# A streaming-encoder block on eight cores: the last down projection in two token ranges, and the wait for the stores moved behind the last branch

## The chip, the cores and the metric

The kernel runs on all 8 cores of one Trainium2 chip. Each core computes one of eight batch elements, with no exchange between cores. The metric is the device time of the slowest core, in microseconds (us). In code and profile lines PE is TensorE, PEld its weight loads, DVE VectorE, ACT ScalarE, POOL GpSimd and SP SyncE; a q behind the name means the engine's queue.

The program has a slow state: in some executions the cores of one die, or of both, get a lower clock, and the time rises by up to 19% (the kernel before once took 3316.71 us). All comparisons here use fast runs. Where I compare cores, I use only dies whose four cores all had a granted clock of 0.99 or more; I call these undisturbed.

## The reference, cut to what matters

```python
# x: (8, 4096, 1024) float32
x = x + 0.5 * swiglu(rmsnorm(x, norm_ffn1), ...)         # first feed-forward half
x = x + merged_attention_and_gating(rmsnorm(x, norm_mix)) @ w_out
x = x + 0.5 * swiglu(rmsnorm(x, norm_ffn2), w_gate, w_up, w_down)
return rmsnorm(x, norm_final)                            # g * x * rsqrt(mean(x*x) + eps)
```

Each core takes its 4096 tokens in 8 tiles of 512. For the last tile nothing is left after the second feed-forward but the final norm and the stores.

## The kernel before, the parts concerned

The program is recorded as a list of operations for each engine. A tracker keeps, for each named resource, its last writer and readers, and turns conflicts into semaphore waits. The resource of the residual is `("X", buffer, d)`: 128 features of all 512 tokens.

```python
def nsq(t, d, eng="pool"):         # squares, summed over the 8 feature blocks
    ... ACT Square -> TG;  eng: ACC += TG  (d == 7: DVE, ACCR = ACC + TG)
def nstat():                       # sum over features, then rsqrt as exp(-0.5 ln)
    ... PE ONESR.T @ ACCR -> psum; ACT Ln -> RSTD; ACT Exp -> RSTD
def napply(t, which, d):           # DVE: X = X * g * RSTD
def store(t, d):                   # SP: rows d and d+1 of X to DRAM

def down(t, i, fac, hook, ...):
    for d in range(8):
        W, wres, k = get_slot(("wds", i, d))
        by = dense_bank()                      # one of four PSUM banks
        ... 22 matmuls of 512 columns into bank(by)
        ... DVE: X[d] = bank(by) * fac + X[d]
        free_slot(k)
        hook()                                 # here nsq(t, d)

# the end of the fast path
run_all(ffn(t, 1, False, ffn2_hooks(t)))
if last:
    nstat()
    for d in range(8):
        napply(t, 3, d)
        if d % 2:
            store(t, d - 1)
outs = [("outd", d) for d in range(0, 8, 2)]
p.add("sp", lambda e: e.nop(), reads=outs)     # SyncE waits for the stores here
p.branch(cond, ["FLI"])                        # every engine reads a flag; if the fast path
...                                            # was not valid, a general version runs
```

The arm after the branch is normally not taken, but all its instructions lie between the branch and the end of the program. So each engine ends with a jump over them. Below, the evict of a block is the VectorE instruction that adds its PSUM bank to the residual (the line with `* fac`), and the issue of a store is the moment at which its queue sends it off.

Of the kernel before, what the change touches and what calls it, by code (L numbers as in the profile page):

```python
# [10 lines left out]
AF = mybir.ActivationFunctionType  # L11
ALU = mybir.AluOpType
# [5 lines left out]
T = 512  # L18
NT = S_LEN // T
NGR = 46  # L20
NSEM = 12
EPS = 1e-6
R_MAX = 1e18
BIAS_MAX = 10.0
# [36 lines left out]
class Prog:  # L61
    ENGS = ("pe", "act", "dve", "pool", "sp")

    def __init__(self, nc):
        self.nc = nc
        self.ops = {e: [] for e in self.ENGS}
        self.last_writer = {}
        self.readers = {}
        self.dma_counts = {}

    @staticmethod
    def _halves(keys):
# [47 lines left out]
    def dma(self, queue, fn, reads=(), writes=(), sem=None, paced=False):  # L120
# [10 lines left out]
        self.ops[queue].append(op)  # L131
        return op

    def branch(self, cond, reads):

        for e in self.ENGS:
            op = _Op(e, cond)
            op.branch = True
            op.idx = len(self.ops[e])
            self._track(op, reads, ())  # L140
            self.ops[e].append(op)

    def emit(self):
        nc = self.nc
        for e in self.ENGS:
            c = 0
            for op in self.ops[e]:
                if not op.is_dma:
                    op.semkey = ("eng", e)
                    if op.signal:  # L150
                        assert not op.branch
                        c += 1
                        op.count = c
        semkeys = [("eng", e) for e in self.ENGS] + [("dma", k) for k in self.dma_counts]
        with ExitStack() as st:
            sems = {k: st.enter_context(nc.semaphore("s_" + "_".join(str(x) for x in k))) for k in semkeys}
            block = st.enter_context(nc.Block())
            engmap = {"pe": block.tensor, "act": block.scalar, "dve": block.vector,
                      "pool": block.gpsimd, "sp": block.sync}

            def make(e):
                def body(eng):
                    waited = {}
                    with ExitStack() as arm:
                        for op in self.ops[e]:
                            for d in op.deps:
                                if waited.get(d.semkey, 0) >= d.count:
                                    continue
                                eng.wait_ge(sems[d.semkey], d.count)
                                waited[d.semkey] = d.count  # L170
                            if op.branch:
                                arm.enter_context(eng.If(op.fn(eng)))
                                continue
                            inst = op.fn(eng)
                            if op.is_dma:
                                inst.then_inc(sems[op.semkey], 16)
                            elif op.signal:
                                inst.then_inc(sems[op.semkey], 1)
                return body

            for e in self.ENGS:
                if self.ops[e]:
                    engmap[e](make(e))
# [19 lines left out]
def build_nc(n_tiles=NT):  # L203
# [28 lines left out]
    with ExitStack() as st:  # L232
# [5 lines left out]
        def bank(i):  # L238
            return PS[i // 2][:, (i % 2) * 512:(i % 2 + 1) * 512]

        def rb(i):
            return ("ps", i)
# [53 lines left out]
        def run(p, dry):  # L296
# [85 lines left out]
            def free_slot(k):  # L382
                if not dry:
                    del live[k]
                    pump()
# [14 lines left out]
            def dense_bank():  # L400
                b = dn[0] % n_dense[0]
                dn[0] += 1
                return b
# [60 lines left out]
                p.add("dve", lambda e: e.memset(EB[64:128, h0:h0 + 2, 0:64], 0.0), reads=[("EB", i)], writes=[("EB", i)])  # L464
                p.add("dve", lambda e: e.memset(EB[0:64, h0:h0 + 2, 576:640], 0.0), reads=[("EB", i)], writes=[("EB", i)])

            def nsq(t, d, eng="pool"):
                src, xres = X[t % 3][:, d, :], ("X", t % 3, d)
                if d == 0:
                    p.add("act", lambda e: e.activation(out=ACC[:], in_=src, func=AF.Square, scale=1.0 / 32.0),  # L470
                          reads=[xres], writes=["ACC"])
                    return
                buf, bres = tg_buf()
                p.add("act", lambda e: e.activation(out=buf[:], in_=src, func=AF.Square, scale=1.0 / 32.0),  # L474
                      reads=[xres], writes=[bres])
                if d < 7:
                    p.add(eng, lambda e: e.tensor_tensor(out=ACC[:], in0=ACC[:], in1=buf[:], op=ALU.add),  # L477
                          reads=["ACC", bres], writes=["ACC"])
                else:
                    p.add("dve", lambda e: e.tensor_tensor(out=ACCR[:], in0=ACC[:], in1=buf[:], op=ALU.add),  # L480
                          reads=["ACC", bres], writes=["ACCR"])

            nb = [0]

            def nstat(dst=RSTD[:], dres="RSTD"):
                b = 6 + nb[0] % 2
                nb[0] += 1
                p.add("pe", lambda e: e.matmul(bank(b), lhsT=ONESR[:], rhs=ACCR[:], start=True, stop=True),
                      reads=["ACCR", "ONESR"], writes=[rb(b)])
                p.add("act", lambda e: e.activation(out=dst, in_=bank(b), func=AF.Ln, bias=EPSB[:]),  # L490
                      reads=[rb(b), "EPSB"], writes=[dres])
                p.add("act", lambda e: e.activation(out=dst, in_=dst, func=AF.Exp, scale=-0.5),  # L492
                      reads=[dres], writes=[dres])

            def napply(t, which, d):
                xres = ("X", t % 3, d)
                src = X[t % 3][:, d, :]
                dst, dres = (XT[t % 2][:, d, :], ("XT", t % 2, d)) if which < 3 else (src, xres)
                p.add("dve", lambda e: e.scalar_tensor_tensor(  # L499
                    out=dst, in0=src, scalar=G4[:, which * 8 + d:which * 8 + d + 1], in1=RSTD[:], op0=ALU.mult, op1=ALU.mult),  # L500
                    reads=[xres, "RSTD", "G4"], writes=[dres])

            def nraw(t, which, d):
# [1 line left out]
                    out=XT[t % 2][:, d, :], in0=X[t % 3][:, d, :], scalar1=G4[:, which * 8 + d:which * 8 + d + 1],  # L505
                    scalar2=None, op0=ALU.mult), reads=[("X", t % 3, d), "G4"], writes=[("XT", t % 2, d)])

            def store(t, d):
                b = t % 3
                p.dma("sp", lambda e: e.dma_start(out=out_d[:, d:d + 2, t * T:(t + 1) * T], in_=X[b][:, d:d + 2, :]),  # L510
                      reads=[("X", b, d), ("X", b, d + 1)], writes=[("outd", d)], sem=f"o{d}")

            N_FFN = 2 * NFC + 16

# [115 lines left out]
                        hook()  # L630
                        yield

            def ffn(t, i, use_tanh, hooks=None, narrow=False):
                hook = Hooks(hooks)
                for f2 in F2:
                    yield from gu_chunk(t, f2, get_slot(("ffs", i, f2)), "tanh" if use_tanh else "silu", hook)
                yield from down(t, i, 0.25 if use_tanh else 0.5, hook, narrow=2 * narrow)

            def gate_up_both(hooks):

# [382 lines left out]
            def ffn2_hooks(t):  # L1023
                hk = {}
                if t + 1 < n_tiles:
                    for s in range(4):
                        add_hook(hk, 8 + 3 * s, P(sgu_mix, t + 1, s))
                if t + 2 < n_tiles:
                    for d in range(8):
                        add_hook(hk, 10 + 3 * d, P(nsq, t + 2, d, "dve" if t == 0 else "pool"))  # L1030
                    add_hook(hk, 40, nstat)
                    for d in range(8):
                        add_hook(hk, D1 + d, P(napply, t + 2, 0, d))
                if t == n_tiles - 1:
                    for d in range(8):
                        add_hook(hk, 4 + 2 * d, P(nsq, t - 1, d))
                    finish_hooks(hk, t - 1, 22)
                    add_hook(hk, 38, flag_ops)
                if t != n_tiles - 2:
                    for d in range(8):  # L1040
                        add_hook(hk, D1 + 2 * d + 1, P(nsq, t, d))
                return hk

            def run_all(g):
                for _ in g:
                    pass
# [29 lines left out]
            for t in range(n_tiles):  # L1076
# [32 lines left out]
                if t == n_tiles - 2:  # L1109
                    last_ffn = ffn(t, 1, True, ffn2_hooks(t), narrow=True)  # L1110
                    interleave(last_ffn, attention(t + 1), N_FFN + 16 - 8, n_att(t + 1), 2 * NFC)
                else:
                    run_all(ffn(t, 1, False, ffn2_hooks(t)))
                    if last:
                        nstat()
                        for d in range(8):
                            napply(t, 3, d)
                            if d % 2:
                                store(t, d - 1)
                    else:  # L1120
                        pass
            outs = [("outd", d) for d in range(0, 8, 2)]
            p.add("sp", lambda e: e.nop(), reads=outs)

            def cond(e):
                r = e.alloc_register("flag")
# [109 lines left out]
```

## Time and profile before

| | us |
|---|---|
| listed runs before the change | 3316.71, 2795.04, 2960.86 (the first and third in the slow state) |
| its profiled execution | 2789.63, cores' spans 2777.5 to 2786.6 |
| first matmul of the last down projection to end of span, median of cores | 57.7 |
| of that, the projection itself | 38.4 |
| last matmul to last store's issue | 11.4 |
| last store's issue to end of span | 7.9 |

The span runs from a core's first to its last recorded instruction. The last four rows are my local measure and its parts, taken from the trace of the profiled execution on all eight cores; it varies by some 0.3 us between most cores, while whole spans of undisturbed cores differ by about 3 us (standard deviation). The local measure starts at the first weight load of the projection. The lines of the profile that carry the reading stand in the prediction.

### The profile page before, as it was taken

How to read it: one execution, taken by the hardware profiler on the slowest of the kernel's cores; microseconds unless marked ns; L12 is line 12 of the kernel's file. 1: busy time of each engine (PE TensorE's matmuls, PEld its weight loads, DVE VectorE, ACT ScalarE, POOL GpSimd, SP SyncE). 2: the span in 40 equal slices, each digit the busy share in tenths (PEclk: the TensorE clock that was granted, in tenths of full speed). 3: DMA queues.
4: the chain of work that ended last, by engine and by line, in shares of the span. 5: the costliest groups of instructions: out<-in, count | busy, mean ns of one | idle time of the engine just before them, and what ended most of it. 6: DMA issues, size and time to landing. Idle time of an engine off the chain costs nothing.

```text
span 2786.6 us, 38337 instructions; the slowest of 8 cores (2777.5 to 2786.6 us)
## 1 busy us (share of the span) xinstructions
PE 2702.4 (97%) x13034; PEld 1209.5 (43%) x13034; DVE 1183.2 (42%) x1940; ACT 910.7 (33%) x1466; POOL 311.5 (11%) x356
## 2 busy tenths in 40 slices
PE   7998999999999999999999999999999999999997
PEld 2443444434444444444444444444444444444343
DVE  5643543435334453344533445424443244455332
ACT  3323432225322353223432244322442225314321
POOL 2001120101111011110011001010011101100111
PEclk9999999999999999999999999999999999999998
DMA  9868989977797556974344634446344453443352
GB/s 190 188 124 178 212 179 178 201 241 149 185 202 222 166 144 175 231 231 148 133 151 144 212 129 136 152 149 210 122 142 150 159 169 130 144 148 123 119 186 79
DMA packets 87124, 461.91 MB, mean 166 GB/s; under 512 B 9224, under 2 KB 9224, under 8 KB 55056
## 3 DMA queue, kind: packets, MB, share of 16 engines
q1 hardware_dynamic: 70656, 365.68, 38.6%
q0 software_dynamic: 16128, 93.69, 21.1%
q8 instruction: 112, 1.84, 0.3%
q14 instruction: 84, 0.69, 0.1%
q10 hardware_dynamic: 144, 0.02, 0.0%
HBM read 488.03 MB, written 65.01 MB: 198 GB/s over the span
## 4 chain that ended last, share of the span: by engine, by line
PE 88%; DMA 5%; DVE 3%; ACT 2%; issue 2%; DVEq 0%; SPq 0%; POOL 0%; ACTq 0%; POOLq 0%
PE ps L547 40%; PE ps L618 19%; PE ps L930 8%; PE ps L671 6%; PE ps L684 4%; PE ps L940 4%; PE ps L959 4%; PE ps L835 2%; DMA ffs<-RING 2%; PE ps L812 1%; ACT E L818 1%; DMA RING<-fsrc 1%; DMA RING<-wd 1%; DMA RING<-ffs 1%; DMA X<-xT 1%
## 5 line engine op out<-in xcount | busy, mean ns | idle before, releaser
L547 PE MATMUL ps<-XT,RING 128*128 128x512 bf16 x5632 | 1232.5, 380 | 25.4 <-DMA RING<-fsrc 10.6
L547 PEld LDWEIGHTS ps<-XT,RING 128*128 128x128 bf16 x5632 | 547.6, 98 | 691.8 <-issue 41.3
L618 PE MATMUL ps<-HT,RING 128*128 128x512 bf16 x2656 | 607.6, 380 | 9.2 <-DVE HT L571 7.1
L477 POOL TENSOR_TENSOR ACC<-ACC,TG 128x512 f32<-128x512 f32 x174 | 224.2, 1289 | 1710.0 <-ACT TG L474 1709.6
L571 DVE TENSOR_TENSOR HT<-ps,TG 128x512 bf16<-128x512 f32 x332 | 229.2, 690 | 386.6 <-PE ps L547 338.9
L618 PEld LDWEIGHTS ps<-HT,RING 128*128 128x128 bf16 x2656 | 252.9, 98 | 317.4 <-issue 36.3
L474 ACT ACTIVATE TG<-X 128x512 f32<-128x512 f32 x224 | 140.1, 627 | 404.0 <-DVE X L624 329.5
L930 PE MATMUL ps<-XT,RING 128*128 128x512 bf16 x1024 | 241.9, 379 | 2.8 <-ACT TG L935 1.6
L554 ACT ACTIVATE TG<-ps 128x512 f32<-128x512 f32 x154 | 91.9, 597 | 402.0 <-PE ps L547 372.6
L560 ACT ACTIVATE TG<-ps 128x512 f32<-128x512 f32 x154 | 91.9, 597 | 372.6 <-PE ps L547 366.3
L556 DVE SCALAR_TENSOR_TENSOR TG<-TG,ps 128x512 f32<-128x512 f32 x154 | 105.8, 687 | 246.7 <-ACT TG L554 201.2
L823 DVE TENSOR_TENSOR E<-E,EB 128x1024 bf16<-128x1024 bf16 (+1 forms) x240 | 120.1, 504 | 168.3 <-ACT E L818 157.7
L624 DVE SCALAR_TENSOR_TENSOR X<-ps,X 128x512 f32<-128x512 f32 x128 | 88.3, 690 | 239.2 <-PE ps L618 238.0
L818 ACT ACTIVATE E<-ps 128x1024 bf16<-128x1024 f32 (+3 forms) x156 | 152.5, 983 | 67.2 <-PE ps L812 62.8
L671 PE MATMUL ps<-XT,RING 128*128 128x512 bf16 x768 | 168.4, 379 | 0.0
L944 DVE SCALAR_TENSOR_TENSOR TG<-TG,ps 128x512 f32<-128x512 f32 x128 | 87.2, 686 | 159.4 <-PE ps L940 122.9
L930 PEld LDWEIGHTS ps<-XT,RING 128*128 128x128 bf16 x1024 | 98.5, 98 | 127.1 <-issue 12.9
L935 ACT ACTIVATE TG<-ps,BG 128x512 f32<-128x512 f32 x128 | 87.2, 687 | 194.9 <-PE ps L930 182.8
L499 DVE SCALAR_TENSOR_TENSOR XT<-X,G,RSTD 128x512 bf16<-128x512 f32 x176 | 124.6, 745 | 36.3 <-ACT RSTD L492 36.3
L671 PEld LDWEIGHTS ps<-XT,RING 128*128 128x128 bf16 x768 | 75.2, 98 | 90.6
L684 PE MATMUL ps<-RING,XT 128*128 128x512 bf16 x512 | 114.3, 379 | 0.0
L959 PE MATMUL ps<-HT,RING 128*128 128x512 bf16 x448 | 99.0, 379 | 2.1 <-DVE HT L949 2.1
(101 smaller groups left out, 1524.4 us busy)
## 6 DMA issues: line engine op xcount, KB each, us to landing
RING<-ffs SPq DMA_DIRECT2D x126, 1024.0 KB, 4.9
RING<-wds SPq DMA_DIRECT2D x93, 704.0 KB, 4.8
RING<-fsrc POOLq DMA_DIRECT2D x38, 1024.0 KB, 14.7
RING<-mgs SPq DMA_DIRECT2D x48, 768.0 KB, 4.2
RING<-wis SPq DMA_DIRECT2D x32, 1024.0 KB, 4.8
RING<-wd POOLq DMA_DIRECT2D x35, 704.0 KB, 13.8
ffs<-RING SPq DMA_DIRECT2D x22, 1024.0 KB, 12.9
out<-X SPq DMA_DIRECT2D x32, 512.0 KB, 5.5
```

Of the source, the lines that this page charges most:

```text
L474: p.add("act", lambda e: e.activation(out=buf[:], in_=src, func=AF.Square, scale=1.0 / 32.0), reads=[xres], writes=[bres])
L477: p.add(eng, lambda e: e.tensor_tensor(out=ACC[:], in0=ACC[:], in1=buf[:], op=ALU.add), reads=["ACC", bres], writes=["ACC"])
L499: p.add("dve", lambda e: e.scalar_tensor_tensor(out=dst, in0=src, scalar=G4[:, which * 8 + d:which * 8 + d + 1], in1=RSTD[:], op0=ALU.mult ...
L547: p.add("pe", lambda e: e.matmul(bank(b), lhsT=Wc[:, kc * 512 + j * 128:kc * 512 + (j + 1) * 128], rhs=xt[:, kc, :], start=(kc == 0), stop ...
L571: p.add("dve", lambda e: e.tensor_tensor(out=dst, in0=bank(bu), in1=buf[:], op=ALU.mult), reads=[rb(bu), bres], writes=[dres])
L618: p.add("pe", lambda e, fc=fc, W=W, by=by, hap=hap: e.matmul(bank(by), lhsT=W[:, fc * 128:(fc + 1) * 128], rhs=hap, start=(fc == 0), stop= ...
L671: p.add("pe", lambda e, kc=kc, W=W, b=b, cc=cc: e.matmul(bank(b), lhsT=W[:, kc * 512 + cc * 128:kc * 512 + (cc + 1) * 128], rhs=XT[t % 2][ ...
L684: p.add("pe", lambda e, kc=kc, W=W, b=b, s=s: e.matmul(bank(b), lhsT=XT[t % 2][:, kc, s * 128:(s + 1) * 128], rhs=W[:, kc * 512:(kc + 1) * ...
L818: p.add("act", lambda e, j=j, sl=sl, qa=qa, col=ok_col(): e.activation(out=E[:, sl, :, qa:T], in_=PS[1 + j][:].rearrange("p (h c) -> p h c ...
L823: p.add("dve", lambda e, sl=sl, q0=q0, q1=q1, u0=u0: e.tensor_tensor(out=E[:, sl, :, q0:q1], in0=E[:, sl, :, q0:q1], in1=EB[:, 2 * hp:2 * ...
L930: p.add("pe", lambda e, kc=kc, W=W, bgt=bgt, j=j: e.matmul(bank(bgt), lhsT=W[:, j * 1024 + kc * 128:j * 1024 + (kc + 1) * 128], rhs=XT[t % ...
L959: p.add("pe", lambda e, dc=dc, W=W, by=by, d4=d4: e.matmul(bank(by), lhsT=W[:, (d4 * 8 + dc) * 128:(d4 * 8 + dc + 1) * 128], rhs=m[:, dc, ...
```

## The change

Its intent is to fill the idle end. The last down projection runs its feature blocks 2 to 7 first on tokens 0 to 319 and then on tokens 320 to 511, so that the final norm and the stores of the first range can go beside the second. SyncE waits for the stores only after the jump. Cut to its core:

```diff
+T_A = 320
+    def end_wait(self, eng, reads):
+        self.last[eng] = [self.last_writer[r] for r in reads]
 ...
+                    for d in self.last.get(e, ()):      # after the branch's arm is closed
+                        eng.wait_ge(sems[d.semkey], d.count)
 ...  (nsq, nstat, napply and store take a slice of tokens; keys of X stay as they were)
+            def down_last(t, i, fac):
+                parts = (slice(0, T_A), slice(T_A, T))
+                ...
+                for d in range(2):
+                    block(d, ALL)
+                    nsq(t, d)
+                for d in range(2, 8):
+                    block(d, parts[0])
+                    nsq(t, d, "dve" if d > 5 else "pool", parts[0])
+                for d in range(2, 8):
+                    block(d, parts[1])
+                    if d == 2:
+                        nstat(sl=parts[0])
+                    nsq(t, d, "dve" if d > 5 else "pool", parts[1])
+                    if d > 2:
+                        for j in range(2):
+                            if 2 * (d - 3) + j < 8:
+                                napply(t, 3, 2 * (d - 3) + j, parts[0])
+                        if d < 7:
+                            store(t, 2 * (d - 3), parts[0])
+                nstat(sl=parts[1])
+                for d in range(8):
+                    napply(t, 3, d, parts[1])
+                    if d % 2:
+                        store(t, d - 1, parts[1], ("sp", "act")[d // 2 % 2])
 ...
-            outs = [("outd", d) for d in range(0, 8, 2)]
-            p.add("sp", lambda e: e.nop(), reads=outs)
+            outs = [("outd", d, h) for d in range(0, 8, 2) for h in range(2)]
+            p.end_wait("sp", outs)
```

## The prediction

> **What bounds the kernel now.** I read the list of cores first, then the share of each engine, then the end of the span in the stretch table, the timeline and the waits of SyncE, because the change touches only the last microseconds.
>
> ```profile
> span 2786.6 us, 38337 instructions; the slowest of 8 cores (2777.5 to 2786.6 us)
> ...
> PE 2702.4 (97%) x13034; PEld 1209.5 (43%) x13034; DVE 1183.2 (42%) x1940; ACT 910.7 (33%) x1466; POOL 311.5 (11%) x356
> ```
>
> TensorE is busy for 97%, and all eight cores run within 9 us of each other at clocks of 0.993 to 0.996. Nothing here shortens that body. The change can win only what lies behind the last matmul. Three stretches of that end, with busy time and count for PE, PEld, DVE, ACT, POOL, then clock, DMA share, GB/s:
>
> ```profile
> 2750.00:2760.00 10.00, 10.00 (x48) 4.57 (x47) 1.38 (x2) 1.26 (x2) 2.98 (x3) 1.00 0.00 1
> 2760.00:2770.00 10.00, 7.43 (x34) 3.15 (x32) 2.08 (x3) 1.26 (x2) 1.82 (x2) 0.99 0.00 1
> 2770.00:2787.00 17.00, 0.24 (x1) 0.00 (x0) 5.39 (x8) 2.60 (x3) 0.00 (x0) 0.50 0.35 128
> ```
>
> So some 19 us pass with TensorE all but idle. The timeline gives the steps:
>
> ```profile
> 2728.86 38.15 PE L618 MATMUL ps<-HT,RING 128*128 128x512 bf16 x176
> ...
> 2767.12 0.69 DVE L624 SCALAR_TENSOR_TENSOR X<-ps,X 128x512 f32<-128x512 f32 x1 [4.06 <-PE ps L618]
> 2768.01 0.63 ACT L474 ACTIVATE TG<-X 128x512 f32<-128x512 f32 x1 [4.12 <-DVE X L624]
> 2768.74 0.69 DVE L480 TENSOR_TENSOR ACCR<-ACC,TG 128x512 fp32r<-128x512 f32 x1 [0.94 <-ACT TG L474]
> ...
> 2769.58 0.66 PE L488 MATMUL ps<-ACCR,ONESR 128*128 128x512 f32 x1 [2.57 <-DVE ACCR L480]
> 2770.32 1.28 ACT L490 ACT_TABLE_LOAD   x1 [1.68 <-PE ps L488]
> 2771.62 0.69 ACT L490 ACTIVATE RSTD<-ps,EPSB 128x512 f32<-128x512 f32 x1
> 2772.39 0.63 ACT L492 ACTIVATE RSTD<-RSTD 128x512 f32<-128x512 f32 x1
> 2773.14 5.39 DVE L499 SCALAR_TENSOR_TENSOR X<-X,G,RSTD 128x512 f32<-128x512 f32 x8 [3.70 <-ACT RSTD L492]
> 2774.63 4.35 SPq L510 DMA_DIRECT2D out<-X  x4
> ```
>
> Every step waits for the one above it. The last matmul ends at 2767.0 and the span at 2786.56: the tail is 19.55 us. Then the waits of SyncE's queue from 2768 on:
>
> ```profile
> SPq L169 <- DMA out<-X: 4.0, 3, 2.0
> ```
>
> The last store goes out at 2778.61. SyncE waits until 2783.1 for the stores, and only then loads the flag (0.47 us) and takes the branch: the trace's records have its compare at 2783.77 and its next instruction at 2786.31, 2.5 us later. From last issue to end: 7.95 us.
>
> **What the Trainium skill says.** "Runtime: NRT & Kernel Launch", section Instruction fetch mechanics: a taken branch to a target outside the fetched window waits for a fetch. The trace agrees: the same jump takes 2.5 us on SyncE and 2.8 us on ScalarE (compare 2772.98, next 2775.80). "ScalarE: Activation LUTs", section Table sets: Ln and Exp share a set, and section What ACT_TABLE_LOAD costs: about 1283 ns a load; the trace has 1.28 us, one load ahead of the pair. The 224 squares of L474 show no load of their own, so a second Ln/Exp after squares should need none. "TensorE: Matmul & The Clock Gate", section Back-to-back issue gap: N/2.4 + 2.5 ns alone, and a sustained 81 ns at N=128 where each matmul has its own weights. The trace agrees with the first, 38.15 us / 176 = 216.8 ns; its runs of attention matmuls, each with own weights, start 109 ns apart at 256 columns and 56 at 128, but are only two to four long. These are durations there, 53 ns less per 128 columns:
>
> ```profile
> L835 PE MATMUL ps<-E,VR 128*128 128x384 bf16 x120 | 32.4, 326 | 0.0
> ...
> L835 PE MATMUL ps<-E,VR 128*128 128x256 bf16 x120 | 18.3, 273 | 0.0
> ```
>
> **The change, part by part.** The last down projection keeps blocks 0 and 1 at 512 tokens; blocks 2 to 7 run first on tokens 0 to 319, then again on 320 to 511. The final norm of the first range is laid between blocks of the second pass.
>
> *TensorE.* 132 matmuls of 512 columns become 132 of 320 (135.8 ns) and 132 of 192 (82.5 ns): 218.3 against 216.8, or 215.8 by the formula, hence 0.3 us more. One more statistics matmul: around L488 the stream loses 236 ns at 512 columns, about 0.2 us here. It stands behind block 2 of the second pass, 1.8 us of matmuls, while its input needs evict, square and add (about 0.5 us each) and handoffs, some 2.0 us plus the 0.3 us drain: TensorE waits about 0.4 us. Sum: the last matmul ends 0.9 us later.
>
> *Sizes.* ScalarE falls 0.835 ns per column (L818: 1016 ns at 1024, 375 at 256), so at 192 columns the square takes 0.36, Ln 0.42, Exp 0.36. VectorE: 690 ns at 512, 350 at 128 (L762), 0.885 ns per column, so 0.41 at 192; the final multiplies come every 0.66 us now, so every 0.38.
>
> *Tail of the second range alone.* Saved against now: evict 0.28, square 0.27, add 0.28, statistics matmul 0.3 (estimate), Ln 0.27, Exp 0.27, eight multiplies 8 x 0.29 = 2.3; sum 3.97. The table load, 1.28 us, moves to the first range's norm, off the end.
>
> *Branch.* SyncE's branch now runs while the stores fly, and it waits afterwards. But stores 2 and 4 of the second range go out on ScalarE's queue, and the last of all is ScalarE's: issue 0.4, flag load 0.5, handoffs 0.2, jump 2.8, final barrier 0.25 = 4.15 us after issue. Its landing is sooner. Of a 512 KB store, 1.2 us looks fixed (0.86 to the first packet, the rest receipt) and 2.6 to 3.4 moves data, since the last four land after 3.8 to 4.6 us; at 192 KB that is 2.2 to 2.5. So 7.95 becomes 4.15: 3.8 saved.
>
> *A new wait.* This I found in the order of the changed build. Dependencies are kept per 512-token row of X, not per range. The evict of block 7, second range, therefore waits for the first range's store of rows 6 and 7, issued just before it, although it writes other tokens. VectorE's order around it is evict 6, add 6 (waits for a square), multiplies 6 and 7 of the first range, then this evict. From the end of block 6: 0.1 + 0.41 + 0.56 + 0.51 + 1.1 = 2.7 us, or 0.9 after the end of block 7. Issue 0.1 later; a 320 KB store lands 2.8 to 3.3 us on by the scaling above. So the evict starts some 4.0 us after the last matmul instead of 0.1.
>
> *Sum.* Tail: 19.55 - 3.97 - 1.28 - 3.8 + 4.0 = 14.5 us. With 0.9 us more of TensorE, the kernel gains about 4 us, 0.15%.
>
> **The rivals.**
> One: the false wait costs nothing, because the store lands while VectorE is still at earlier work. Then the gain is 8 us. Against it: VectorE has only some 1.4 us of work per 1.8 us block and catches up; and the last four landings of the kernel before took no less than 3.8 us.
> Two: narrow matmuls run at the pace of weight loads (PEld shows 98 ns each), not 82.5. Then 132 x 15.5 ns = 2.0 us are lost and the gain is 2 us. For it: the trace has no long run of 192 columns. Against: loads there start 56 ns apart while each takes 98, so they overlap.
> Three: ScalarE's jump or a straggling DMA queue takes 1 to 2 us more, or the first norm's table load makes the squares late and the second pass stalls on PSUM banks. Gain 1 to 3 us. Against the stall: four banks give three blocks, 5.5 us, of slack, the norm blocks ScalarE for about 3.
> Four: none of it can be seen. Two undisturbed executions of before stand at 2789.63 and 2795.04 us, 5.4 apart, more than the whole gain.
>
> **Range and chances.** The tail is 0.7% of the span, so even removing all 19.5 us would not reach 2%. A slowdown over 2% needs 56 us, which nothing here can cost. The listed median, 2960.86 us, and the highest, 3316.71, come from the chip's slow state; my number is for a fast run. The two undisturbed values average 2792; less 4 gives 2788. The gain lies between 1 and 9 us, and executions scatter by 0.3%, 8 us: range 2776 to 2800. Chance of within 2%: 0.97; faster 0.02, slower 0.01.
>
> **What would show it right or wrong.** In the changed profile: (1) matmuls of 192 columns in runs of 22 in 1.8 us, not 2.2; (2) one table load in the last 40 us after the gate and up work, ahead of the first range's Ln, none ahead of the second's; (3) the evict of block 7 idle for about 3 us or more after its matmuls, released by the store of rows 6 and 7; (4) eight multiplies in about 3.1 us; (5) an end about 4 us after the last issue, ScalarE's jump the last thing before the final barrier; (6) from last matmul to end 14.5 us instead of 19.55. A tail near 10 us means the false wait is hidden; one of 17 or more means the branch or the landing did not shorten. If the fast times fell by over 10 us, something outside the tail moved, and my account would be wrong.

## The result, and the profile after

The first comparison gave 2785.97, 2785.52, 2786.33 and 2791.52 us in fast runs (and 2886.09 in the slow state), against fast runs of 2795.04 and 2798.13 before: ratio 0.9967, 95% interval 0.9943 to 0.9991. That is 9 us less. All ratios in this document are the mean time of one kernel's fast runs over that of the other's fast runs of the same rounds, so not quite the ratio of medians.

The page of the kernel after, slowest core:

```profile
span 2784.3 us, 38428 instructions; the slowest of 8 cores (2775.6 to 2784.3 us)
...
PE 2691.5 (97%) x12911; PEld 1222.0 (44%) x13167; DVE 1186.6 (43%) x1957; ACT 912.2 (33%) x1474; POOL 311.6 (11%) x359
```

As foretold, the body is unchanged. (There are 12911 matmul records beside 13167 weight loads: some matmul records are missing, so I take the phase from the weight loads and the last matmul.) The timeline of the same core (start in us, duration in us, engine, line, operation, count, and the idle time before with what ended it):

```profile
2730.07 29.41 PE L659 MATMUL ps<-HT,RING 128*128 128x512 bf16 x197
...
2759.67 0.38 PE L500 MATMUL ps<-ACCR,ONESR 128*128 128x320 f32 x1 [0.20 <-DVE ACCR L491]
...
2759.90 9.25 PE L659 MATMUL ps<-HT,RING 128*128 128x192 bf16 x110
2760.14 1.28 ACT L502 ACT_TABLE_LOAD   x1 [1.21 <-PE ps L500]
2761.43 0.53 ACT L502 ACTIVATE RSTD<-ps,EPSB 128x320 f32<-128x320 f32 x1
...
2772.35 0.36 DVE L664 SCALAR_TENSOR_TENSOR X<-ps,X 128x192 f32<-128x192 f32 x1 [2.60 <-DMA out<-X]
2772.91 0.36 ACT L485 ACTIVATE TG<-X 128x192 f32<-128x192 f32 x1 [4.54 <-DVE X L664]
2773.38 0.36 DVE L491 TENSOR_TENSOR ACCR<-ACC,TG 128x192 fp32r<-128x192 f32 x1 [0.67 <-ACT TG L485]
...
2773.88 0.50 PE L500 MATMUL ps<-ACCR,ONESR 128*128 128x192 f32 x1 [4.74 <-DVE ACCR L491]
2774.76 0.42 ACT L502 ACTIVATE RSTD<-ps,EPSB 128x192 f32<-128x192 f32 x1 [1.48 <-PE ps L500]
2775.27 0.36 ACT L504 ACTIVATE RSTD<-RSTD 128x192 f32<-128x192 f32 x1
2775.73 2.73 DVE L511 SCALAR_TENSOR_TENSOR X<-X,G,RSTD 128x192 f32<-128x192 f32 x8 [2.00 <-ACT RSTD L504]
2777.22 1.70 ACTq L523 DMA_DIRECT2D out<-X  x2
```

The matmuls end at 2769.15. The evict of block 7 starts at 2772.35: its 2.60 us of idle time were ended by a store (`DMA out<-X`), not by its matmuls. That is the false wait: the store reads the first range of the row, the evict writes the second. From there on each step is shorter than its partner before (0.36 for 0.69, 0.42 for 0.69, 2.73 for 5.39), and the table load stands at 2760.14, beside matmuls. The last issue is at 2778.54, on ScalarE's queue.

The medians of the eight cores:

| us, median of cores | before | after | difference |
|---|---|---|---|
| projection, first weight load to last matmul's end | 38.36 | 39.29 | +0.93 |
| last matmul to last store's issue | 11.42 | 9.43 | -1.99 |
| last store's issue to end of span | 7.87 | 4.63 | -3.24 |
| sum, the local measure (medians, so not exactly the sum) | 57.72 | 53.40 | -4.3 |

So the traces show 4.3 us and the first ratio says 9. The experiments ask where the rest is, and whether the parts are what I took them for.

### The profile page after: what moved, and what is told of

Same layout as the page of the kernel before. It is cut to its first block, busy times and chain, and to the rows that moved or that the text cites. A ratio compares the mean times of both kernels' runs of the same rounds, so it can differ in the third digit from the quotient of the medians.

```text
span 2784.3 us, 38428 instructions; the slowest of 8 cores (2775.6 to 2784.3 us)
## 1 busy us (share of the span) xinstructions
PE 2691.5 (97%) x12911; PEld 1222.0 (44%) x13167; DVE 1186.6 (43%) x1957; ACT 912.2 (33%) x1474; POOL 311.6 (11%) x359
## 4 chain that ended last, share of the span: by engine, by line
PE 90%; DVE 3%; issue 3%; ACT 2%; DMA 1%; POOL 0%; SPq 0%; DVEq 0%; ACTq 0%; POOLq 0%
PE ps L560 42%; PE ps L631 18%; PE ps L993 8%; PE ps L734 5%; PE ps L747 4%; PE ps L1003 4%; PE ps L1022 4%; PE ps L898 2%; PE ps L659 1%; PE ps L875 1%; ACT E L881 1%; DMA X<-xT 1%; DVE X L637 1%; DVE E L886 1%; ACT TG L907 0%
## 5 line engine op out<-in xcount | busy, mean ns | idle before, releaser
L631 PE MATMUL ps<-HT,RING 128*128 128x512 bf16 x2417 | 564.6, 381 | 14.5 <-DVE HT L584 7.8
L488 POOL TENSOR_TENSOR ACC<-ACC,TG 128x512 f32<-128x512 f32 (+2 forms) x177 | 224.3, 1267 | 1703.6 <-ACT TG L485 1702.8
L631 PEld LDWEIGHTS ps<-HT,RING 128*128 128x128 bf16 x2480 | 236.1, 98 | 299.2 <-issue 40.0
L485 ACT ACTIVATE TG<-X 128x512 f32<-128x512 f32 (+2 forms) x230 | 141.3, 616 | 403.8 <-DVE X L637 300.6
L1022 PE MATMUL ps<-HT,RING 128*128 128x512 bf16 x440 | 98.5, 379 | 2.5 <-DVE HT L1012 2.1
```

The source lines that it names most:

```text
L485: p.add("act", lambda e: e.activation(out=buf[:, sl], in_=src, func=AF.Square, scale=1.0 / 32.0), reads=[xres], writes=[bres])
L488: p.add(eng, lambda e: e.tensor_tensor(out=acc, in0=acc, in1=buf[:, sl], op=ALU.add), reads=["ACC", bres], writes=["ACC"])
L631: p.add("pe", lambda e, fc=fc, W=W, by=by, hap=hap: e.matmul(bank(by), lhsT=W[:, fc * 128:(fc + 1) * 128], rhs=hap, start=(fc == 0), stop= ...
L1022: p.add("pe", lambda e, dc=dc, W=W, by=by, d4=d4: e.matmul(bank(by), lhsT=W[:, (d4 * 8 + dc) * 128:(d4 * 8 + dc + 1) * 128], rhs=m[:, dc, ...
```

## The experiments

Two theories at the start. **A**: the tail is all that moved, and the first ratio was sampling. **B**: something outside the tail moved too. Within the tail there was a rival for each part: that the false wait costs nothing because the stores or jumps end last anyway; that the jump is bound by ScalarE in any case; that narrow matmuls run at the pace of the weight loads.

### again: the changed kernel unaltered, more rounds

> The changed kernel itself, more rounds, on the same chip as the next three. Local measure in the profile: from the first matmul of the last down projection to the end of the span, median of cores; 57.5 us before, 53.2 us changed. Theory A (the tail is all that moved): ratio of fast runs near 0.9985 (4.3 us), local measure again 53.2. Theory B (something ahead of the tail moved too, as the first ratio 0.9967 suggests): ratio again near 0.9967 (9 us), and the time up to the last down projection shorter than before on the median of the cores by some 5 us.

Measured: ratio 0.9994 (0.9950 to 1.0039), spoiled by one run of 2805.34 us in which two cores had a clock of 0.982 and 0.983, yet not slow enough to be counted as slow. The undisturbed runs average 6.1 us (standard error 1.2) below those of before in the same job, the spans of single undisturbed cores 4.4 us (0.7). Local measure: 53.28. The time up to the projection: 2724.8 on the median against 2724.6 before. So nothing ahead of the tail moved, and theory B in that form falls. (The time up to the projection alone would not show it: the same changed kernel had 2728.5 in the first comparison and 2726.1 in again_b. That the spans fell by no more than the local measure does.) But the slowest-core time fell by more than the spans, and that was not yet explained.

### branch_only: the kernel before with only the wait moved

```diff
-            p.add("sp", lambda e: e.nop(), reads=outs)
+            p.end_wait("sp", outs)
```

> The kernel before with only the wait for stores moved behind the branch. Theory A: flag load and jump of SyncE, 3.2 us, are hidden behind the landing of 4.5 us: from last issue to end 7.9 becomes 4.7, local measure 57.5 becomes 54.3, ratio 0.9989. Rival (jumps of several engines fetch at once and slow each other, or the jump slows the stores): 5.5 or more from issue to end, local measure over 55.

Measured: ratio 1.0044 (0.9944 to 1.0144), useless as a time, since one disturbed run of 2820.75 us counted as fast; the two undisturbed runs took 2788.46 and 2788.48. Local measure 56.86, last issue to end 7.07. Only 0.9 us were gained where theory A said 3.2. The landing was as before (4.26 us after issue). In the trace's records of SyncE on the slowest core the jump is done at 2784.44, three of the four waits follow within 0.14 us, and the fourth passes at 2786.47, 1.9 us later, although its store had landed. So neither the landing nor the jump held it. Something between two adjacent wait instructions did.

### before_pad and branch_pad: 64 NOPs in the arm that never runs

Looking for the 1.9 us I compared time with span. In every listed run the kernel before takes 2.9 to 3.4 us longer than the span of its slowest core, and every other kernel so far 1.6 to 1.75. Both could be a fetch of the next block of instructions. NOPs in the arm not taken cost no time and only shift what follows:

```diff
             p.branch(cond, ["FLI"])
+            for _ in range(64):
+                p.add("sp", lambda e: e.nop())
```

> The kernel before with 64 NOPs on SyncE inside the arm that is never taken, so that only the place of SyncE's last instructions among the fetched blocks moves. In all 12 listed runs the kernel before takes 3.05 us more than the span of its slowest core, every other kernel so far 1.65 to 1.75, and only its trace has a second instruction fetch, 2.4 us after the last instruction. Theory (that fetch is on the path by accident of placement and accounts for 1.4 us of the measured gain): time minus span falls to 1.7, local measure stays at 57.7, ratio 0.9995. Rival (the 1.4 us has another cause): 3.05 stays.

> The kernel with only the wait moved behind the branch, and 64 NOPs on SyncE in the arm not taken. In branch_only the fourth wait of SyncE came 1.9 us after the third although its store had landed, with an instruction fetch in between. Theory (the end of a fetched block fell between the two waits): last issue to end 7.07 becomes 5.0, local measure 56.9 becomes 54.8. Rival (the jump and the waits cost that much by themselves): 7.0 stays.

Measured: before_pad has 1.52 to 1.65 us between span and time in all six runs, where the kernel before kept 2.97 to 3.44 in its eleven runs of that job. Its local measure is 57.75, unchanged. Its ratio of 1.0005 (0.9982 to 1.0027) contains a disturbed run of 2805.94; its four undisturbed runs are 2.6 us (0.9) below those of before. The queue of instruction fetches (q14: packets, MB, share of 16 engines) after the end of the span, kernel before:

```profile
q14 instruction: 2, 0.02, 0.4%
```

and the same stretch of before_pad:

```profile
q14 instruction: 1, 0.01, 0.2%
```

One fetch less. These are the slowest cores; in the traces all eight cores of the kernel before start a fetch 2.4 to 2.9 us after the end of their span, and none of before_pad does. branch_pad: local measure 54.91, last issue to end 5.13, and its four waits pass within 0.18 us. In the stretch from 2778 us to the end of the span, branch_only fetches four times,

```profile
q14 instruction: 4, 0.03, 1.2%
```

and branch_pad three times:

```profile
q14 instruction: 3, 0.02, 1.8%
```

Both theories hold. NOPs that never run add no work; they only shift SyncE's last instructions among the fetched blocks. Their place there decides whether one more fetch, 1.4 to 1.9 us, stands in the way. In the kernel before it lies behind the span, in branch_only inside it; in the changed kernel the gap between span and time is 1.6 to 1.75 us and no core's waits lie more than 0.4 us apart. So 1.4 us of the measured gain come from a shift of the code that nobody intended. Moving the wait alone is worth 2.8 us (57.72 to 54.91) once the accident is out of it; ratio of branch_pad 0.9983 (0.9969 to 0.9996).

### wait_back: the changed kernel with the wait ahead of the branch

```diff
-            p.end_wait("sp", outs)
+            p.add("sp", lambda e: e.nop(), reads=outs)
```

> The changed kernel with the wait for stores put back ahead of the branch. If the jump is hidden in the changed kernel: SyncE ends 3.2 us plus 0.3 after the landing of the last store (3.7 to 4.2 us after issue), so from last issue to end 4.6 becomes about 7.3, local measure 53.2 becomes 55.9. Rival (ScalarE's jump bounds in any case): under 1 us more.

Measured: last issue to end 7.37, local measure 56.07, ratio 0.9989 (0.9971 to 1.0006). The wait stands on the path again; the waits of SyncE's queue from 2768 us on show it (total us, times, longest):

```profile
SPq L175 <- DMA out<-X: 4.0, 4, 2.0
```

The changed kernel has no such line in that stretch. The jump hidden there is worth 2.7 us. ScalarE's own jump does not bind in any case: the rival falls.

### split_keys: dependencies of X by token range

```diff
-            if k[0] == "TG" and len(k) == 2:
+            if (k[0] == "TG" and len(k) == 2) or (k[0] == "X" and len(k) == 3):
+            def xk(b, d, sl):
+                return ("X", b, d) if sl == ALL else ("X", b, d, int(sl.start > 0))
 ...  (nsq, napply, store and the evict of down_last use xk)
```

> The changed kernel with the dependencies of X kept for each token range, so that the evict of block 7 no longer waits for the store of the other range. Theory (the false wait is on the path): the 2.6 us idle of that evict goes, last matmul to end 14.1 becomes 11.5, local measure 53.2 becomes 50.6, ratio to before 0.9975. Rival (the time comes back in the landing of the stores or the jumps, which are what ends last): less than 1 us.

Measured: local measure 50.34, last matmul to last issue 6.53 instead of 9.43; ratio 0.9965 (0.9948 to 0.9983). The timeline of its slowest core:

```profile
2767.76 1.90 PE L662 MATMUL ps<-HT,RING 128*128 128x192 bf16 x21
...
2769.25 1.01 DVE L514 SCALAR_TENSOR_TENSOR X<-X,G,RSTD 128x320 f32<-128x320 f32 x2
2770.18 0.35 DVE L667 SCALAR_TENSOR_TENSOR X<-ps,X 128x192 f32<-128x192 f32 x1
...
2773.38 2.72 DVE L514 SCALAR_TENSOR_TENSOR X<-X,G,RSTD 128x192 f32<-128x192 f32 x8 [1.83 <-ACT RSTD L507]
```

The last evict follows the two multiplies at once, with no idle time before it, 0.5 us after the matmuls' end at 2769.66. The false wait was on the path, and its 3 us do not come back: from last issue to end it is 4.52 as against 4.63.

### table_early: the table of Ln and Exp loaded early, in the kernel before

```diff
+                if t == n_tiles - 1:
+                    add_hook(hk, D1 + 1, lambda: p.add(
+                        "act", lambda e: e.activation(out=DUM[:], in_=EPSB[:], func=AF.Ln), reads=["EPSB"], writes=["DUM"]))
```

> The kernel before with one Ln of one column on ScalarE at the start of the last down projection, so that the table of Ln and Exp is loaded there. Theory (the load is on the path of the tail and squares do not take the table away): no load ahead of the last Ln, local measure 57.7 becomes 56.4. Rival: squares reload, or the 1.3 us comes back elsewhere, 57.5 or more.

Measured: last matmul to last issue 10.14, exactly 1.28 less than 11.42; local measure 56.74, since from issue to end it took 8.17 instead of 7.87 in this one execution. ScalarE's timeline of the slowest core:

```profile
2732.85 1.28 ACT L1042 ACT_TABLE_LOAD   x1
2734.14 0.20 ACT L1042 ACTIVATE DUM<-EPSB 128x1 f32<-128x1 f32 x1
...
2774.88 0.69 ACT L491 ACTIVATE RSTD<-ps,EPSB 128x512 f32<-128x512 f32 x1 [1.51 <-PE ps L489]
```

The last Ln needs no load, with eight squares between. The load was on the path; of its 1.28 us, 0.98 stayed in the local measure. (The one timed run has 3.33 us between span and time, and all eight cores have the late fetch: without the NOPs this kernel keeps what the kernel before has.)

### ta384: with split_keys, 384 tokens in the first range and 128 in the second

```diff
-T_A = 320
+T_A = 384
```

> The kernel with dependencies by range and 384 tokens in the first range, 128 in the second. If the steps of the tail scale with the columns: 0.06 us less in each of six steps and 8 x 0.06 in the multiplies, 0.8 us; matmuls at 162.5 + 55.6 ns keep their sum. Local measure 50.3 becomes 49.5. Rival (second pass too short: blocks of 1.2 us against 1.4 us of VectorE work, or weight loads bind at 128 columns): 50.3 or more.

Measured: local measure 52.66, ratio 0.9968 (0.9955 to 0.9982): the rival is right that it is no gain, and its first reason, a second pass that is too short, fits; its second, weight loads, does not. TensorE's groups in the stretch from 2725 us on:

```profile
L662 PE MATMUL ps<-HT,RING 128*128 128x128 bf16 x132 | 7.7, 219 | 0.0
...
L503 PE MATMUL ps<-ACCR,ONESR 128*128 128x384 f32 x1 | 0.4, 412 | 1.0 <-DVE ACCR L494 1.0
```

132 matmuls of 128 columns, each with its own weights, are busy for 7.7 us, 58 ns each. Instead, TensorE stood for 1.0 us (0.2 in the changed kernel) before the first range's statistics, because one block of 128 columns, 1.2 us, is too short to cover the evict, square and add of the larger range. And with six blocks of 1.2 us VectorE fell behind: the last issue came 7.62 us after the last matmul, not 6.53. My expectation had counted the steps of the tail and not the pace of the pass.

### fill: in split_keys, the multiplies of the first range ahead of the add

```diff
-                    nsq(t, d, "dve" if d > 5 else "pool", parts[1])
                     if d > 2:
                         ... napply(t, 3, 2 * (d - 3) + j, parts[0])
+                    nsq(t, d, "dve" if d > 5 else "pool", parts[1])
```

> Split dependencies, and in the second pass the multiplies of the first range stand ahead of the add of squares on VectorE, so that they fill its wait for the square. In split_keys the evict of block 7 starts 0.5 us after its matmuls, behind two multiplies. Theory: it starts 0.1 us after them; last matmul to last issue 6.53 becomes 6.1, local measure 50.3 becomes 49.9, ratio 0.996. Rival: the add of block 6 comes later by as much, nothing gained, 50.3.

Measured: last matmul to last issue 6.12, as expected; local measure 50.14, since issue to end was 4.72 this time; ratio 0.9959 (0.9946 to 0.9972). Its timeline at block 7:

```profile
2768.91 0.35 DVE L491 TENSOR_TENSOR ACC<-ACC,TG 128x192 f32<-128x192 f32 x1
2769.52 0.36 DVE L667 SCALAR_TENSOR_TENSOR X<-ps,X 128x192 f32<-128x192 f32 x1 [0.27 <-PE ps L662]
```

The add has no idle time any more and the evict waits for TensorE alone. That 0.4 us is clear in the step but 0.2 in the local measure, and no time shows it: fill took 2780.90 to 2785.66, split_keys 2781.27 to 2783.64 in another job. Both beat the kernel before and the changed one.

### fill_sp: all stores of the second range on SyncE

```diff
-                        store(t, d - 1, parts[1], ("sp", "act")[d // 2 % 2])
+                        store(t, d - 1, parts[1])
```

> The same with all stores of the second range on SyncE. Theory (a jump of about 3.3 us after the last issue bounds the end, whichever queue has it): last issue to end 4.5 becomes about 4.9, since SyncE has eight waits (0.4 us) after its jump where ScalarE had none, local measure plus 0.4. Rival (ScalarE's jump ran beside SyncE's and slowed both): 4.2 or less.

Inconclusive. Last issue to end was 5.01 on the median, near the 4.9 of theory, but the cores fall into two groups, four at 4.35 to 4.48 and four at 5.54 to 6.01, and one die was disturbed (clock 0.984). Each group has two cores of either die, so the clock does not part them; SyncE's jump does, with 2.6 to 2.8 us in the one and 3.7 to 4.3 in the other, though ScalarE's jump was over in both. Whether the second queue pays is left open.

### again_b: the changed kernel beside fill

> The changed kernel once more, beside fill on one chip. With tail gain 4.3 us and 1.4 us from the fetch after the end, undisturbed runs stand 5.7 us below those of before (ratio 0.998), and fill 3.4 us below the changed kernel. If the first ratio 0.9967 was right, 9 us.

Measured: ratio 0.9975 (0.9962 to 0.9988), 7.5 us (1.1) below the undisturbed runs of before in the job, local measure 53.20. fill was 4.6 us below it there (2782.6 against 2787.2 on average), expected 3.4.

### All of them side by side

Differences to the kernel before of the same job. There were three jobs, each on its own chip: again, branch_only, wait_back and split_keys; before_pad, branch_pad, table_early and ta384; fill, fill_sp and again_b. In them the undisturbed runs of the kernel before average 2791.9, 2792.7 and 2794.7 us. Compare rows of one job. Spans: mean over all undisturbed cores of all runs; time: mean over runs with both dies undisturbed; standard errors in brackets.

| kernel | local measure | spans of cores | time of slowest core |
|---|---|---|---|
| changed (again) | -4.4 | -4.4 (0.7) | -6.1 (1.2) |
| changed (again_b) | -4.5 | -5.0 (0.6) | -7.5 (1.1) |
| branch_only | -0.9 | -1.0 (0.7) | -3.5 (1.0) |
| branch_pad | -2.8 | -3.3 (0.6) | -4.9 (1.3) |
| wait_back | -1.7 | -1.9 (0.6) | -3.2 (1.2) |
| before_pad | 0.0 | -0.2 (0.6) | -2.6 (0.9) |
| split_keys | -7.4 | -7.5 (0.6) | -9.3 (1.1) |
| ta384 | -5.1 | -6.1 (0.6) | -8.7 (0.8) |
| fill | -7.6 | -8.7 (0.6) | -12.1 (1.2) |

The second column follows the first. The third is lower by about 2 us for every kernel, even for before_pad, whose instructions that run are those of before. 1.4 us of that is the fetch after the span. The rest, up to 1.2 us for most rows and 2 for the last, is about one to two standard errors and stays unexplained.

## Why the prediction was right or wrong

**The time.** 2788 was predicted for a fast run, 2776 to 2800 as range; the changed kernel's undisturbed runs took 2784.86 to 2791.52. Within 2% was right.

**The gain** was too small in the prediction: 4 us, against 9 in the first comparison and 6.1 and 7.5 in the later ones. The step that failed is the last of the sum, "Tail: 19.55 - 3.97 - 1.28 - 3.8 + 4.0 = 14.5 us. With 0.9 us more of TensorE, the kernel gains about 4 us". As a sum for the span it comes out right, 4.3 us on the median of cores, tail 14.11, but partly by luck: the new wait was put 0.8 us too high and the branch's saving 0.6 us too high, and the two nearly cancel. (It also adds 4.0 us for the new wait where its own text, 4.0 instead of 0.1, gives 3.9.) And it lets the time end with the span. The term that is missing is the instruction fetch behind it, 1.4 us in the kernel before and gone in the changed one. Nothing in the views that I read shows it; a comparison of the time with the longest span did (3.0 us against 1.7). 4.3 + 1.4 = 5.7, which the later comparisons meet within 0.4 and 1.8 us. Some 3.5 us of the first comparison's 9 are in no part that an experiment shows; that cause stays open. The likeliest is sampling: the 9 rested on two fast runs of before, 2795.04 and 2798.13, average 2796.6, while its 25 undisturbed runs in the three later jobs average 2793.4.

**TensorE**: right. +0.93 us against 0.9. The 110 matmuls of 192 columns take 9.25 us, less a drain of 0.25 and over 109 intervals 82.6 ns, predicted 82.5; so rival two falls, and with it the stall on PSUM banks that rival three named. Only the wait before the first statistics was 0.2 us and not 0.4.

**Narrow steps and table load**: right. From the start of the last evict to the last issue: 11.31 us before, 6.18 after on the median of cores, 5.13 saved; predicted 3.97 + 1.28 = 5.25. Two small misses cancel in it: on the slowest cores the eight multiplies took 2.73 us and not 3.1, but from the evict to the first multiply 2.64 were saved (6.02 to 3.38) and not 1.67 + 1.28. table_early showed the load alone at 1.28.

**The new wait**: right in kind, over-sized. Predicted to move the evict to 4.0 us after the last matmul; it was 3.2 (2772.35 less 2769.15 on the slowest core), because the 320 KB store went out 0.7 us after the last matmul and not 1.0, and landed 2.3 us after its issue and not 2.8 to 3.3. Taking the wait away gave 2.9 us up to the last issue, so rival one, that the store lands behind other work anyway, falls.

**The branch**: the right path, but 3.24 us saved against 3.8; the term that was too small is the jump, put at 2.8 us. On two of eight cores the end came 5.7 to 5.9 us after the last issue instead of 4.4 to 4.7. The jump of ScalarE takes 3.0 to 3.5 us on six cores of the changed kernel and 4.4 and 4.7 us on the two that ended late, against 2.6 to 2.8 before, where it fell mostly ahead of the stores. The two late cores are of that one execution: in again and again_b all sixteen end 4.2 to 4.9 us after the last issue. Nor is ScalarE's jump always the last thing: on four of the eight cores SyncE's last wait passed after it. That jumps slow each other by fetching at once fits (rival three), but was not tested by itself, and it can't be all: in branch_only SyncE's jump took 3.1 to 3.5 us with ScalarE's long over (2.5 to 2.8 in the kernel before). The stores in flight are another candidate; this stays open.

The last landing was mis-sized too: the last store of 192 KB lands 3.8 us after its issue and not 2.2 to 2.5. Size is not what decides, since the first of the four, just as large, lands after 2.25 to 2.39. On the median the jump hides it, so it did little harm.

**Rival four**, that it can't be seen, fell: the intervals of the first comparison and of again_b are clear of 1. That of the run called again was not, because of one disturbed run.

## What to carry to other kernels

When a tile is cut in parts to overlap its end, cut the dependency keys as well, and look in the built order for waits on a store of the other part: here it cost 3 of a possible 7.4 us. Hide a taken branch behind the landing of the stores; that is worth 2.7 us here, but check that no fetch of the next instruction block falls into the last waits, by comparing the time with the longest span and by adding NOPs where they never run. For a change of 0.2% read the part that changed on every core of the trace; the time of the slowest core needed some ten runs to say the same less clearly.

## What the Trainium skill lacked or had wrong

- "Runtime: NRT & Kernel Launch", Instruction fetch mechanics: it calls the crossing of a block's boundary mostly hidden. After a taken jump it is not: 1.9 us between two waits in branch_only, 1.4 us after the span in the kernel before, both gone with 64 NOPs (1.52 to 1.65 us between span and time, from 2.97 to 3.44). The page gives no time for a taken jump that has to fetch; here 2.4 to 4.7 us on SyncE and ScalarE from the compare to the next instruction. ("Advanced Engine Details and Errata", Control Flow Timing, has only a compare-and-branch of some 108 ns, and does not speak of a fetch.)
- "TensorE: Matmul & The Clock Gate", Back-to-back issue gap: it gives a sustained 81 ns for 128 columns and 131 ns for 512 where each matmul has its own weights. Here 132 such matmuls of 128 columns (ta384) are busy for 7.7 us, 58 ns each, and 176 of 512 columns take 216.8 ns each. Its formula for the gap alone, N/2.4 + 2.5 ns, fits these streams: 82.6 ns measured at 192 columns, 82.5 by the formula.
- "ScalarE: Activation LUTs", What ACT_TABLE_LOAD costs: it adds a drain of some 1380 ns to the load of 1283. In the tail before, the load takes 1.28 us and Ln starts 0.02 us after it; taking the load away gave 1.28 us, so no drain was on the path.
